# One descriptor per partition for every load of a streaming row normalizer

## The chip, the cores and the metric

The kernel runs on one core of one Trainium2 chip. The metric is the device time of one execution in microseconds (us), lower is better. TensorE is not used. The core's 16 DMA engines carry all traffic between HBM and SBUF.

## The reference

Every row of 1024 numbers is divided by the sum of its absolute values. There are 32 x 512 = 16384 rows, 64 MiB in and 64 MiB out.

```python
batch, seq, dim = 32, 512, 1024
sums = np.sum(np.abs(x), axis=-1, keepdims=True)
return (x / (sums + 1e-8)).astype(np.float32)
```

## The kernel before

The 16384 rows are laid over 128 partitions, 128 rows for each partition, and cut into 11 tiles. Tiles 0 to 9 hold 12 rows per partition: 12 x 4 KB = 48 KB per partition and 6144 KB in all. Tile 10, the last, holds 8 rows per partition: 32 KB and 4096 KB in all. The rows that one partition gets of one tile lie one after another in HBM, so a tile's row of bytes in a partition is one unbroken run on both sides.

`sbuf` has four buffers of the full tile size (`BUFS = 4`). A tile is loaded into a buffer, worked on in place and stored from it. So load i+4 needs the buffer of tile i, and has to wait until store i has landed in HBM.

The order is written out by hand. SyncE's queue (SP) issues all loads, ScalarE's queue (ACT) issues all stores:

```python
for i in range(BUFS):
    load(i)
for i in range(len(rows)):
    compute(i)
    store(i)
    if i + BUFS < len(rows):
        load(i + BUFS)
```

`compute(i)` calls `normalize`. VectorE (DVE) sums the absolute values of each row (line 47), adds the epsilon (line 54), takes the reciprocal (line 56) and multiplies the tile by it (line 58, all rows in one instruction). In tiles 0, 1, 2, 9 and 10 some rows are instead multiplied one at a time, by VectorE (line 65) or by ScalarE (line 68); the table `split` says how many.

`load` (line 86) and `store` (line 89) are one `dma_start` each. Their argument `max_dma_last_dim` is the largest number of bytes that one DMA descriptor may carry. A descriptor is the order for one contiguous run. With `WHOLE` = 49152 bytes a full tile is 128 descriptors of 48 KB, one for each partition. With `HALF` = 24576 bytes it is 256 descriptors of 24 KB, two for each partition. The last tile's 32 KB per partition are one descriptor of 32 KB with `WHOLE`, and two of 16 KB with `HALF`. Every DMA is spread evenly over the 16 engines, 8 partitions for each, so an engine gets 8 or 16 descriptors of each DMA.

Before the change, loads 0 and 1 use `WHOLE` and loads 2 to 10 use `HALF`; stores 0 to 8 use `HALF` and stores 9 and 10 use `WHOLE`.

In the profile q1 is the DMA queue of the loads and q10 that of the stores. What the profile calls a packet is one descriptor; each DMA also has one packet of 4 bytes on each engine, which reports its completion.

Of the kernel before, what the change touches and what calls it, by code (L numbers as in the profile page):

```python
# [1 line left out]

# [4 lines left out]

FP32 = mybir.dt.float32
EPS = 1e-8


@with_exitstack
def kernel(
    ctx: ExitStack,
    tc: tile.TileContext,
    x: bass.AP,
    out: bass.AP,
):
    nc = tc.nc
    P = nc.NUM_PARTITIONS  # L20

    x_flat = x.flatten_outer_dims()
    out_flat = out.flatten_outer_dims()
    n, d = x_flat.shape

    R = 12
    BUFS = 4
    HEAD = 32
    per_partition = n // P
    assert n % P == 0 and (per_partition - HEAD) % R == 0  # L30
    rows = [R] * ((per_partition - HEAD) // R + 2) + [HEAD - 2 * R]

    def piece(flat, i):
        head = flat[: P * HEAD, :].rearrange("(p r) d -> p r d", p=P)
        if i < 2:
            return head[:, R * i : R * (i + 1), :]
        if i == len(rows) - 1:
            return head[:, 2 * R :, :]
        a = P * (HEAD + R * (i - 2))
        return flat[a : a + P * R, :].rearrange("(p r) d -> p r d", p=P)  # L40

    sbuf = ctx.enter_context(tc.tile_pool(name="sbuf", bufs=BUFS))
    stats = ctx.enter_context(tc.tile_pool(name="stats", bufs=len(rows)))

    def normalize(x_tile, k, kv, kt):
        s = stats.tile([P, R], FP32)
        nc.vector.tensor_reduce(  # L47
            out=s[:, :k],
            in_=x_tile[:, :k, :],
            axis=mybir.AxisListType.X,  # L50
            op=mybir.AluOpType.add,
            apply_absolute_value=True,
        )
        nc.vector.tensor_scalar_add(out=s[:, :k], in0=s[:, :k], scalar1=EPS)  # L54
        inv = stats.tile([P, R], FP32)
        nc.vector.reciprocal(out=inv[:, :k], in_=s[:, :k])  # L56
        if kv:
            nc.vector.tensor_mul(  # L58
                out=x_tile[:, :kv, :],
                in0=x_tile[:, :kv, :],  # L60
                in1=inv[:, :kv].unsqueeze(2).to_broadcast([P, kv, d]),
            )
        for r in range(kv, kv + kt):
            row = x_tile[:, r, :]
            nc.vector.tensor_scalar_mul(out=row, in0=row, scalar1=inv[:, r : r + 1])  # L65
        for r in range(kv + kt, k):
            row = x_tile[:, r, :]
            nc.scalar.activation(  # L68
                out=row,
                in_=row,  # L70
                func=mybir.ActivationFunctionType.Copy,
                scale=inv[:, r : r + 1],
            )

    last = len(rows) - 1
    split = {0: (3, 4), 1: (0, 3), 2: (0, 3), last - 1: (0, 2), last: (5, 3)}

    tiles = {}

    HALF, WHOLE = 24576, 49152

    def load(i):
        x_tile = tiles[i] = sbuf.tile([P, R, d], FP32, name="x_tile")
        nc.sync.dma_start(out=x_tile[:, : rows[i], :], in_=piece(x_flat, i), max_dma_last_dim=WHOLE if i < 2 else HALF)  # L86

    def store(i):
        nc.scalar.dma_start(out=piece(out_flat, i), in_=tiles[i][:, : rows[i], :], max_dma_last_dim=WHOLE if i >= last - 1 else HALF)

    def compute(i):
        k = rows[i]
        kt, ks = split.get(i, (0, 0))
        normalize(tiles[i], k, k - kt - ks, kt)

    with tc.manual_schedule():
# [9 lines that stand above are left out]
# [1 line left out]
_INS = ['x']  # L107
_OUTS = [((32, 512, 1024), 'float32')]


# [23 lines left out]
```

## Time and profile before

| what | value |
|---|---|
| time, median of 3 runs | 316.99 us (316.77 to 317.28) |
| span of the profiled execution, from its first to its last instruction | 315.3 us |
| median less span | 1.7 us |
| VectorE busy | 261.2 us (83%) |
| ScalarE busy | 17.4 us (6%) |
| loaded and stored | 67.11 MB each |
| mean DMA rate over the span | 426 GB/s |

The profile does not give a device time of the profiled execution itself; its span stands for it, and the 1.7 us between the span and the median of the timed runs are taken as the same before and after. Busy shares are of the span. The 40 slices of the page are 7.88 us each. In the slices and windows a packet's whole size and time are booked where it starts, so short windows swing by one packet per engine in each direction, and a share can exceed 1.

### The profile page before, as it was taken

What the parts mean: (1) busy time and instruction counts of PE and PEld (TensorE: products, weight loads), DVE (VectorE), ACT (ScalarE), POOL (GpSimd) and SP (SyncE); (2) the same over time, 40 slices, a digit from 0 to 9 for tenths busy, and PEclk for the clock granted to TensorE, in tenths of its full rate; (3) what the DMA queues carried; (4) which work ended last, traced back from release to release, by engine and by line L of the source; (5) the groups of instructions that cost most, each with busy time, mean ns of one, the idle gap of its engine ahead of it and who ended that gap; (6) DMA issues with size and microseconds to landing.
All of it is one profiled execution on the core that took longest, in us unless ns stands there. A gap on an engine that the chain in (4) does not pass through costs nothing.

```text
span 315.3 us, 168 instructions
## 1 busy us (share of the span) xinstructions
DVE 261.2 (83%) x51; ACT 17.4 (6%) x16; POOL 0.2 (0%) x4
## 2 busy tenths in 40 slices
DVE  0079999999999999979996997999699969999100
ACT  0010403004000000000000000000000000203100
POOL 0000000000000000000000000000000000000000
DMA  8999999999999999999999999999999999999997
GB/s 312 486 399 415 433 396 421 430 446 421 430 449 421 427 449 421 427 449 424 427 446 424 427 446 427 424 446 430 421 446 433 421 442 424 441 423 493 399 416 316
DMA packets 5472, 134.22 MB, mean 426 GB/s; under 512 B 352, under 2 KB 352, under 8 KB 352
## 3 DMA queue, kind: packets, MB, share of 16 engines
q1 hardware_dynamic: 2736, 67.11, 49.9%
q10 hardware_dynamic: 2736, 67.11, 49.4%
HBM read 67.11 MB, written 67.11 MB: 426 GB/s over the span
## 4 chain that ended last, share of the span: by engine, by line
DVE 41%; DMA 33%; another core or an unknown queue 18%; SPq 0%; issue 0%; DVEq 0%
DVE s L47 23%; DMA x_tile<-in_x_dram 17%; DMA out_dram<-x_tile 16%; DVE x_tile L58 15%; DVE x_tile L65 2%; DVE inv L56 0%; DVE s L54 0%; SPq L86 0%; DVEq L129 0%
## 5 line engine op out<-in xcount | busy, mean ns | idle before, releaser
L47 DVE TENSOR_REDUCE s<-x_tile 128x12 f32<-128x12288 f32 (+1 forms) x11 | 138.2, 12563 | 30.1 <-DMA x_tile<-in_x_dram 30.1
L58 DVE TENSOR_TENSOR x_tile<-x_tile,inv 128x12288 f32<-128x12288 f32 (+3 forms) x10 | 113.6, 11358 | 0.5
L68 ACT ACTIVATE x_tile<-x_tile,inv 128x1024 f32<-128x1024 f32 x15 | 16.1, 1139 | 257.2 <-DVE inv L56 257.2
L65 DVE TENSOR_SCALAR x_tile<-x_tile,inv 128x1024 f32<-128x1024 f32 x8 | 5.5, 749 | 0.0
L56 DVE RECIPROCAL inv<-s 128x12 f32<-128x12 f32 (+1 forms) x11 | 2.5, 226 | 0.4
L68 ACT ACT_TABLE_LOAD x1 | 1.3, 1283 | 17.8 <-DMA x_tile<-in_x_dram 17.8
L54 DVE TENSOR_SCALAR s<-s 128x12 f32<-128x12 f32 (+1 forms) x11 | 1.9, 173 | 0.4
L118 POOL MEMSET const-bfloat16-1.0<- 128x1 bf16 x1 | 0.1, 102 | 0.0
L118 POOL MEMSET const-uint8-127<- 128x1 uint8 x1 | 0.1, 102 | 0.0
L118 POOL MEMSET const-float32-0.0<- 128x1 f32 x1 | 0.1, 99 | 0.2 <-issue 0.2
L118 POOL MEMSET const-float32-1.0<- 128x1 f32 x1 | 0.1, 99 | 0.0
## 6 DMA issues: line engine op xcount, KB each, us to landing
x_tile<-in_x_dram SPq DMA_DIRECT2D x10, 6144.0 KB, 37.3
out_dram<-x_tile ACTq DMA_DIRECT2D x10, 6144.0 KB, 47.5
x_tile<-in_x_dram SPq DMA_DIRECT2D x1, 4096.0 KB, 32.5
out_dram<-x_tile ACTq DMA_DIRECT2D x1, 4096.0 KB, 21.5
```

The source lines that it names most:

```text
L47: nc.vector.tensor_reduce(out=s[:, :k], in_=x_tile[:, :k, :], axis=mybir.AxisListType.X, op=mybir.AluOpType.add, apply_absolute_value=True,)
L54: nc.vector.tensor_scalar_add(out=s[:, :k], in0=s[:, :k], scalar1=EPS)
L56: nc.vector.reciprocal(out=inv[:, :k], in_=s[:, :k])
L58: nc.vector.tensor_mul(out=x_tile[:, :kv, :], in0=x_tile[:, :kv, :], in1=inv[:, :kv].unsqueeze(2).to_broadcast([P, kv, d]),)
L65: nc.vector.tensor_scalar_mul(out=row, in0=row, scalar1=inv[:, r : r + 1])
L68: nc.scalar.activation(out=row, in_=row, func=mybir.ActivationFunctionType.Copy, scale=inv[:, r : r + 1],)
L118: nc = _bacc.Bacc("TRN2", target_bir_lowering=False, num_devices=1)
```

## The change

Loads 2 to 10 get `WHOLE` as well, so every load has one descriptor per partition. Stores stay as they are: two descriptors per partition for stores 0 to 8, one for stores 9 and 10. No tile, buffer, instruction of VectorE or ScalarE, or order of issue is touched; the instruction lists of both kernels differ in the nine load instructions alone, whose shape goes from 128x2x6144 to 128x12288 (128x2x4096 to 128x8192 for the last).

```diff
     def load(i):
         x_tile = tiles[i] = sbuf.tile([P, R, d], FP32, name="x_tile")
-        nc.sync.dma_start(out=x_tile[:, : rows[i], :], in_=piece(x_flat, i), max_dma_last_dim=WHOLE if i < 2 else HALF)
+        nc.sync.dma_start(out=x_tile[:, : rows[i], :], in_=piece(x_flat, i), max_dma_last_dim=WHOLE)
```

## Prediction, made before the changed kernel ran

> **What bounds the kernel now.** I read the page's busy shares first, then its slices and queues:
>
> ```profile
> span 315.3 us, 168 instructions
> DVE 261.2 (83%) x51; ACT 17.4 (6%) x16; POOL 0.2 (0%) x4
> ...
> DMA  8999999999999999999999999999999999999997
> GB/s 312 486 399 415 433 396 421 430 446 421 430 449 421 427 449 421 427 449 424 427 446 424 427 446 427 424 446 430 421 446 433 421 442 424 441 423 493 399 416 316
> ...
> q1 hardware_dynamic: 2736, 67.11, 49.9%
> q10 hardware_dynamic: 2736, 67.11, 49.4%
> ```
>
> VectorE is idle for a sixth of the span. The DMA row is 9 in every slice but the first and last, and both queues together take 49.9 + 49.4 = 99.3% of the 16 engines' time. The trace's packet records agree: from the first packet at 1.75 us to the last at 313.84 us each engine's packets follow one another with no gap over 40 ns. The page's chain of waits also ends in DMAs: VectorE takes tile after tile as loads land, and loads wait for stores. But it is a chain through instructions; the stores after VectorE's last instruction (292.6 us) run on to 313.84. So the time is the sum of what each engine must move, as long as some queue always has work.
>
> What does a descriptor cost? The DMA view of four windows tells: loads alone in 48 KB pieces (4 to 16.7 us) and in 24 KB pieces (31 to 36.5), both queues in 24 KB pieces (64 to 247), and the last load's 16 KB pieces beside 24 KB stores (257 to 277). Columns are packets, MB, share of 16 engines:
>
> ```profile
> q1 hardware_dynamic: 112, 5.51, 100.1%
> ```
> ```profile
> q1 hardware_dynamic: 112, 2.36, 99.7%
> ```
> ```profile
> DMA packets 3430, 79.23 MB, mean 433 GB/s; under 512 B 206, under 2 KB 206, under 8 KB 206
> ...
> q1 hardware_dynamic: 1714, 39.76, 50.4%
> q10 hardware_dynamic: 1716, 39.47, 50.1%
> ```
> ```profile
> q10 hardware_dynamic: 217, 4.94, 57.3%
> q1 hardware_dynamic: 222, 3.64, 42.4%
> ```
>
> First window: 1.001 x 16 x 12.7 us / 112 = 1.816 us for 48 KB. Second: 0.997 x 16 x 5.5 / 96 data packets = 0.91 us for 24 KB. Starts of successive packets of one engine in the records are finer: 1.812 us for 48 KB, 1.209 for 32 KB, 0.908 for 24 KB, 0.607 for 16 KB. These are the same alone and beside the other queue. So merging two 24 KB pieces saves 2 x 0.908 - 1.812 = 4 to 5 ns (4.4 in means), and two 16 KB pieces 5 ns.
>
> The last two windows tell the arbitration. Beside each other the queues move equal numbers of packets, even where their sizes differ: 222 to 217 packets, 3.64 to 4.94 MB. In the records an engine alternates strictly, one load descriptor, one store descriptor. The Trainium skill, page "DMA: Bandwidth & Descriptors", section on queues, rings and completion order, says instead that an engine drains a whole ring packet of some 9 to 17 descriptors before it turns to the next queue. By that rule the sizes of descriptors would hardly shift the shares; the rows decide against it, and the end time worked out below is the same by both, since it is a sum over a full pipe.
>
> **The change, part by part.** *Descriptors.* Loads 2 to 9 lose 8 descriptors per engine each, 8 x 8 = 64, at 4.4 ns: 0.28 us. Load 10 loses 8 at 5.2 ns: 0.04. Sum: -0.32 us on every engine, all on the path that sets the end. SP's issue instructions cost nothing: their 0.37 us each lies beside full queues.
>
> *Shares.* With loads at 48 KB against stores at 24 KB, a turn of both is 1.812 + 0.908 = 2.72 us and moves twice as much load as store. A load's 8 descriptors per engine need 8 x 2.72 = 21.8 us, and 8 of the 16 store descriptors pass with them; the other 8 run alone, 7.26 us. Together 29.02 us per tile against 32 x 0.908 = 29.06 now: the saving again, nothing more. Loads land sooner, stores later, in the middle of the run.
>
> *Where the VectorE stalls go.* The page shows what VectorE waits for, and the list of waits what SP waits for:
>
> ```profile
> L47 DVE TENSOR_REDUCE s<-x_tile 128x12 f32<-128x12288 f32 (+1 forms) x11 | 138.2, 12563 | 30.1 <-DMA x_tile<-in_x_dram 30.1
> ...
> x_tile<-in_x_dram SPq DMA_DIRECT2D x10, 6144.0 KB, 37.3
> out_dram<-x_tile ACTq DMA_DIRECT2D x10, 6144.0 KB, 47.5
> ```
> ```profile
> SPq L86 <- DMA out_dram<-x_tile: 227.0, 7, 55.3
> ```
>
> 17.7 us of VectorE's 30.1 are the first load; the other 12.4 are five waits for loads 5 to 9. Load latency falls from 37.3 to about 23 us (21.8 plus about 1 from issue to first packet, as for load 0: 0.73 to 1.75), so those waits should almost go. I carried this through with VectorE's durations of the timeline (a middle tile is 12.95 + 12.96 + 0.5 = 26.4 us). Store 0, issued at 38.8, lands about 76 instead of 73, because it gets a third of the pipe until load 3 is in at about 72. From there load i+4 is issued at 76, 105, 134, 163, 193, 222, 251 and lands 23 us later (18 for the last). VectorE runs from tile to tile and ends near 281 instead of 292.6. Late next is the store queue: stores 8, 9 and 10 are then still to move, and the engines end by the sum.
>
> *Is the pipe always full?* A store must already be issued when the one before lands. Store 1 is issued at 61.9 and store 0 lands at 76: 15 us of cover. Later ones have 20 to 34 us, and store 10, issued near 281, is due near 304. So I charge nothing for it; if the cover were gone, each us of late store would cost a us.
>
> *A price the trace does not show.* Now the load queue never runs dry until the last load: load i+4 is issued about 8 us before the one ahead of it lands (load 5 at 102.1, load 4 lands 110.4). After the change load i+4 is issued some 4 to 6 us after load i+3 has landed, from load 4 on, 7 times: the load queue starts from empty while stores run. The nearest rows are two starts from empty. The first packets of load 0 took 2.45 us and 1.8 to 2.8 in all instead of 1.815, on average 0.64 us lost per engine. And when store 0 joined, the load packets around it took up to 1.9 us instead of 0.912, 0.91 us lost per engine on average (the only such place in the trace); the windows view has it at 40 to 44 us (last column GB/s):
>
> ```profile
> 32.00:40.00 8.00, 8.00 (x5) 3.46 (x4) 0.00 (x0) 1.00 1.01 436
> 40.00:44.00 4.00, 4.00 (x1) 0.00 (x0) 0.00 (x0) 1.00 0.95 313
> ```
>
> A restart can cost from 0 to 0.91 us. I take 0: the engine has store descriptors to run while the new queue's first data are on their way, and the loss at 40 us may belong to the first writes to HBM, which occur once in both kernels; load 0's loss had no other work to cover it. Below zero is excluded, since a full pipe has nothing to give back. The Trainium skill, page "HBM Reference", section Latency, speaks against the change: it gives 0.2 us for an access on average and 2 us at high load. If every restart showed that 2 us in full, 7 of them would be 14 us by an estimate from that page; no row here shows a loss that large.
>
> Sum: 315.3 - 0.32 = 315.0 us of span, and with the 1.7 us around it 316.7.
>
> **The rivals.** *Faster.* The stall at 40 us could shrink too, since half as many load descriptors are in flight when store 0 joins. All of it is 0.91 us: 316.99 - 0.32 - 0.91 = 315.8. For it: it is load packets that stretch there. Against it: bytes in flight are the same. Nothing else on the engines is left to gain, since they have no gaps.
>
> *Slower: restarts of an emptied load queue.* Price 7 x c - 0.32. With c = 0.64 (load 0) it is +4.2, 321.2 us; with c = 0.91 (store 0) +6.1, 323.1. It decides from c = 0.046 us for the sign and from (0.63 + 0.32) / 7 = 0.14 us for a loss above 0.2%. For it: both starts from empty in the trace lose time, the second of them beside a queue that was full. Against it: one had nothing to overlap with, the other was the run's first store.
>
> *The change does nothing:* the first two loads already show packets of 49152 bytes under this setting, so it will act. If not, 317.0.
>
> **How the numbers follow.** A measurement of this kernel can tell about 0.2% (0.63 us) from no change. Full pipe with free restarts, 316.7: 0.47, and no effect 0.02; both within 0.2%. Restarts at 0.14 us or more: 0.40. The stall at 40 us also shrinks enough to pass 0.2%: 0.11. So faster 0.11, same 0.49, slower 0.40. The range goes from the faster rival's 315.8 to the slow one's upper bound, 323.1, and leaves out under 1 in 10; the likeliest case alone is 316.3 to 317.2.
>
> **What would show it.** Right: q1 falls from 2736 packets by 72 x 16 = 1152 to 1584, load latency from 37.3 to near 23 us, VectorE's waits for loads from 30.1 to about 18 to 19 us with its last instruction near 281, load packets of 1.815 us also where stores run, and an end of packets near 313.5. Wrong: packets longer than 1.83 us (load) or 0.92 us (store) after 74, 103 or 132 us, where a load begins again, or slices below 9 in the DMA row.

## The result and the profile after

The changed kernel takes 324.31 us (median of 4 runs, 323.44 to 327.93) against 317.05 us before: a ratio of 1.0253, 95% interval 1.0219 to 1.0288. That is 7.3 us slower, and above the upper end of the predicted range. The profiled execution has a span of 321.9 us, 6.6 us more than before. Its page:

```profile
span 321.9 us, 168 instructions
...
DMA  8999999999999999999999999999999999999993
GB/s 336 446 397 483 391 382 446 421 415 437 440 440 434 428 421 434 425 418 428 437 415 382 440 437 458 388 440 406 437 415 440 409 421 430 428 434 458 417 426 143
...
q1 hardware_dynamic: 1584, 67.11, 49.6%
q10 hardware_dynamic: 2736, 67.11, 48.5%
...
L47 DVE TENSOR_REDUCE s<-x_tile 128x12 f32<-128x12288 f32 (+1 forms) x11 | 138.2, 12561 | 30.9 <-DMA x_tile<-in_x_dram 30.9
...
x_tile<-in_x_dram SPq DMA_DIRECT2D x10, 6144.0 KB, 28.7
out_dram<-x_tile ACTq DMA_DIRECT2D x10, 6144.0 KB, 53.3
```

q1 has the 1584 packets that the change was to bring. The DMA row is still 9 from the second slice to the last but one, so it is not idle time that was added. But the last slice is 3 with 143 GB/s where it was 7 with 316, and loads take 28.7 us to land, not the 23 expected.

The chain of waits shows when it happens. SP issues a load each time a store has landed; each piece called "another core or an unknown queue" here is SP's wait for that store, on this one core:

```profile
106.07 0.33 SPq L86
...
106.47 29.80 another core or an unknown queue
...
136.35 0.33 SPq L86
136.67 30.04 another core or an unknown queue
...
166.78 0.33 SPq L86
167.11 29.59 another core or an unknown queue
...
196.76 0.33 SPq L86
197.09 30.30 another core or an unknown queue
...
227.45 0.33 SPq L86
227.78 29.48 another core or an unknown queue
...
257.31 23.47 DMA x_tile<-in_x_dram
```

Before, these steps were 29.0 to 29.1 us apart:

```profile
160.28 0.37 SPq L86
160.65 28.69 another core or an unknown queue
...
189.41 0.37 SPq L86
189.78 28.58 another core or an unknown queue
...
218.43 37.34 DMA x_tile<-in_x_dram
```

Load 4 is issued at 77.04 and load 5 at 106.07, 29.03 us later, the 29.02 of the sum. The five steps that follow are 30.28, 30.43, 29.98, 30.69 and 29.86 us. Six steps take 180.3 us where the sum had 174.1.

The packet records split the 6.6 us in two. Before, no engine has a gap between packets in the middle of the run; after, a few gaps of under 0.9 us come to about 0.15 us per engine in all. So lost time shows almost only as packets longer than their normal length. Summed over packets after 60 us and divided by 16 engines, this stretch is zero before and 3.36 us after. By load, counted from its issue to the next load's issue:

| load that starts again | 4 | 5 | 6 | 7 | 8 | 9 | 10 |
|---|---|---|---|---|---|---|---|
| lost per engine, mean, us | 0.00 | 0.26 | 0.57 | 1.02 | 0.57 | 0.65 | 0.29 |
| from issue to its first packet, us | 3.56 | 3.57 | 3.81 | 4.33 | 3.40 | 4.05 | 3.54 |

All but 0.03 of the 3.36 us fall between 1.5 us before and 9 us after a load's first packet. The rest of each load, another 12 us or more with the same two to one share of loads and stores, loses nothing.

With 0.3 us more at the two starts that the trace of before has too (load 0, store 0), and 0.32 us less for descriptors, the mean engine ends 3.4 us later: 316.99 after, 313.58 before (times at which the 16 engines complete the last store).

The other half is that the engines lose unequally. At load 5 five of them lose 0.3 to 1.4 us each, the others 0.1 or nothing. Followed from packet to packet (each starts where the one before it on its engine ended), the same five lose most again at load 6 (1.3 to 1.6 us against 0.3 or less) and at load 8 (1.0 to 1.3 us against 0.5 or less). After 60 us they lose 5.7 to 6.6 us each, the other eleven 1.4 to 2.8. Each engine has its own 8 partitions of every tile, and what one falls behind is not made good: store 1 completes on all 16 within 0.5 us, store 3 within 2.9, store 5 within 4.6. Before, the last store's 16 completions lie between 313.27 and 313.83 us; after, between 314.79 and 320.44. The slowest engine is 3.45 us behind the mean, where it was 0.25. Together 3.4 + 3.2 = 6.6 us. The windows view of the end shows the engines dropping out one by one (last two columns: DMA share, GB/s):

```profile
308.00:314.00 6.00, 0.00 (x0) 0.00 (x0) 0.00 (x0) 1.00 1.00 431
314.00:320.00 6.00, 0.00 (x0) 0.00 (x0) 0.00 (x0) 1.00 0.39 169
```

### The profile page after: what moved, and what is told of

It is laid out like the page before. It is cut to its first block, busy times and chain, and to the rows that moved or that the text cites. A ratio compares the mean times of both kernels' runs of the same rounds, so it can differ in the third digit from the quotient of the medians.

```text
span 321.9 us, 168 instructions
## 1 busy us (share of the span) xinstructions
DVE 261.1 (81%) x51; ACT 17.4 (5%) x16; POOL 0.2 (0%) x4
## 3 DMA queue, kind: packets, MB, share of 16 engines
q1 hardware_dynamic: 1584, 67.11, 49.6%
## 4 chain that ended last, share of the span: by engine, by line
another core or an unknown queue 46%; DMA 26%; DVE 17%; SPq 1%; issue 0%; DVEq 0%; ACTq 0%
DMA out_dram<-x_tile 14%; DMA x_tile<-in_x_dram 13%; DVE s L47 11%; DVE x_tile L58 5%; DVE x_tile L65 1%; SPq L86 1%; DVE inv L56 0%; DVEq L129 0%; DVE s L54 0%; ACTq L89 0%
## 5 line engine op out<-in xcount | busy, mean ns | idle before, releaser
L47 DVE TENSOR_REDUCE s<-x_tile 128x12 f32<-128x12288 f32 (+1 forms) x11 | 138.2, 12561 | 30.9 <-DMA x_tile<-in_x_dram 30.9
## 6 DMA issues: line engine op xcount, KB each, us to landing
x_tile<-in_x_dram SPq DMA_DIRECT2D x10, 6144.0 KB, 28.7
```

The costliest lines, as they stand in the source:

```text
L47: nc.vector.tensor_reduce(out=s[:, :k], in_=x_tile[:, :k, :], axis=mybir.AxisListType.X, op=mybir.AluOpType.add, apply_absolute_value=True,)
```

## The experiments

Three theories stood against one another. **A**: a load queue that has run empty and starts again beside running stores costs time. **B**: 48 KB packets beside the other queue's packets stretch by themselves. **C**: the two to one share costs by itself, whether or not the queue ran empty.

**All loads and stores with 48 KB.** Same load packets as the changed kernel, but equal shares, so the load queue never runs empty.

```diff
-        nc.scalar.dma_start(..., max_dma_last_dim=WHOLE if i >= last - 1 else HALF)
+        nc.scalar.dma_start(..., max_dma_last_dim=WHOLE)
```

> Theory A (restart): what costs time is a load queue that has run empty and starts again beside running stores. With 48 KB for loads and stores alike the queues share the engines evenly again, load i+4 is queued about 7 us before the load ahead of it is done, and the load queue never runs empty. Then only the descriptor savings are left: 0.32 us of the loads and as much of stores 0 to 8 (9 x 8 x 4.4 ns), so about 316.3 us, and the engines finish within 1 us of one another. Theory B (size): 48 KB load packets beside another queue's packets are themselves what stretches. Then this kernel has as many of them in the mix and is slow as well, 321 us or more.

317.4 us, ratio 1.0011 (1.0002 to 1.0020). Packets after 60 us are stretched by 0.04 us per engine in all. The DMA view from 64 to 247 us, of the changed kernel first and then of this one (packets, MB, share):

```profile
q10 hardware_dynamic: 1715, 39.79, 50.7%
q1 hardware_dynamic: 870, 38.04, 49.4%
```
```profile
q1 hardware_dynamic: 912, 40.11, 50.6%
q10 hardware_dynamic: 910, 39.32, 49.6%
```

In each, 96 packets of q1 are completions of 4 bytes. So a 48 KB load packet took 0.494 x 16 x 183 / 774 = 1.87 us in the changed kernel and 0.506 x 16 x 183 / 816 = 1.82 us here, its length when alone. B falls. C is not touched, since the shares are equal here too. The 0.64 us expected from fewer descriptors did not show in the time: about 0.5 us of it went into more stretch before 45 us (the loads alone and store 0's joining), and one engine ended 1.0 us behind the mean.

**Half the sizes, same shares.** Loads 24 KB, stores 12 KB:

```diff
-        ... max_dma_last_dim=WHOLE if i >= last - 1 else HALF)   # stores
+        ... max_dma_last_dim=WHOLE if i >= last - 1 else HALF // 2)
```

> Loads 24 KB, stores 0 to 10 12 KB (8 KB in the last): no packet is larger than before, but loads again get twice the share of stores and the load queue runs empty before each of loads 4 to 10. Theory A: as slow as the changed kernel, plus 0.6 us for the 144 or more extra store descriptors per engine at 4.4 ns: about 322 to 328 us, with restarts that lose 0.2 to 1 us each and engines that end some 5 us apart. Theory B: no 48 KB packet stands in the mix, so about 317.8 us.

The diff leaves stores 9 and 10 at 48 and 32 KB; the expectation named them wrongly. 319.33 us, ratio 1.0074 (1.0060 to 1.0088): slower, between the two predictions. The load queue is empty before each of loads 4 to 10 again. The losses are 0, 0.02, 0.26, 0.23, 0.20, 0.27 and 0.32 us, 1.3 us in all, and the engines end within 0.9 us of one another. So a 48 KB packet is not needed for a loss. But restarts cost less than half as much with packets of half the size, and the engines hardly part. A's figure for this run was too high.

**Loads held back.** The sizes of the kernel before, with GpSimd work between a store's landing and the next load, so that the queue should run empty at equal shares; and a control where the load does not wait for that work.

```diff
+        if i >= BUFS:
+            nc.gpsimd.memset(x_tile[:, 0, 0:1], 0.0)
+            for _ in range(DELAY):                    # DELAY = 18
+                nc.gpsimd.memset(pad[:, :], 0.0)      # pad is 128x1024, 0.95 us each
+            nc.gpsimd.memset(x_tile[:, 0, 0:1], 0.0)  # not in the control
```

> Packet sizes and shares of the kernel before, but loads 4 to 10 are held back after the landing of their store by 18 memsets of 128x1024 on the otherwise idle GpSimd (about 10 to 20 us), so that the load queue runs empty before each of them. VectorE still has its tiles in time: stores are queued 20 us ahead. Theory A: seven restarts from empty, 3 to 8 us over before, 320 to 325 us. Theory B, or a theory by which the uneven 2 to 1 share is what costs: within 0.3% of before, 316.5 to 318 us.

> Control for the late loads: the same 18 memsets on GpSimd, but the load waits only for a one-column memset ahead of them, so the load queue is as full as before (as long as GpSimd is done with one batch before the next store lands). Both theories: as before within 0.2%, 316.4 to 317.7 us. If it is slower, GpSimd's writes cost DMA time by themselves and the late-load run has to be read against this one.

Late loads 318.47 us, ratio 1.0050 (1.0033 to 1.0067); control 317.34, 1.0015 (1.0006 to 1.0024). This run did not do what it was made for. With no load beside it, a store lands sooner, the next load is issued sooner, and the loads bunch up: in its profile the load queue was empty before load 4 and, for 2.7 us, before load 8, and the store queue before store 4. None of the three shows a loss (0.02 us per engine up to 285 us). It tells only that a restart can be free, not that it is.

**Part of the change alone.** 48 KB for loads 2 and 3 only, and for loads 2 to 6 only:

```diff
-        ... max_dma_last_dim=WHOLE if i < 2 else HALF)   # loads
+        ... max_dma_last_dim=WHOLE if i < 4 else HALF)   # i < 7 in the second
```

> One part of the change alone: loads 2 and 3 with 48 KB descriptors, loads 4 to 10 with 24 KB as before. Load 3 is in at about 73 us, store 0 lands near 76, so load 4 starts an empty queue; from load 5 on the queue is full again. One restart instead of seven. Theory A: a seventh of the loss or less, 0.2 to 1 us: 317.0 to 318.0 us, losses in packets near 80 us only. Theory C: the share is two to one only from 43 to 72 us, where the changed kernel showed no loss: 316.9 us.

> A larger part: loads 2 to 6 with 48 KB descriptors, loads 7 to 10 with 24 KB. Restarts from empty at loads 4, 5, 6 and 7 (about 80, 110, 139 and 168 us), none after that. Theory A: about four sevenths of the loss of 7 us, 319.5 to 321.5 us, packet losses at these four places and none later, engines 3 to 4 us apart at the end. Theory C: three loads (4 to 6) at two to one, about three sevenths, 319 to 320.5 us, and no loss where load 7 with 24 KB begins.

Two loads: 317.08 us, ratio 1.0008 (0.9998 to 1.0017), one restart, 0.04 us lost there: less than A had expected for a start, and a time that fits A and C alike. Five loads: 320.7 us, ratio 1.0111 (1.0092 to 1.0130), four restarts. They lose 0, 0.18, 0.30 and, at load 7, 0.20 us, then 0.17 us more while load 7 runs, and nothing after 195 us. The slowest engine ends 3.4 us behind the mean. Load 7 has 24 KB packets and an equal share, and its start is as dear as those of loads 5 and 6: that speaks against C. Restarts against time go 0, 1, 4, 7 to 316.9, 317.1, 320.7 and 324 us.

**The gap filled.** The last way is to leave sizes and shares of the changed kernel and keep the load queue from running empty. Behind each of loads 3 to 9 small filler loads are queued, 512 bytes per descriptor, into spare tiles that nobody uses. They take turns with store packets until the next load is there.

```diff
+    def filler(i):                     # after load(i), i = 3 to 9
+        for j, (parts, at) in enumerate(((P, 0), (P // 2, 128))):
+            pad = spare.tile([parts, 128], FP32, name=f"pad{i}_{j}")
+            nc.sync.dma_start(out=pad[:, :], in_=x_flat[:parts, at : at + 128])
```

> The changed kernel, with two small filler loads queued right behind each of loads 3 to 9: 192 descriptors of 512 bytes, 12 on each of eight engines and 8 or more on most, read from the first rows of the input into a spare tile that nobody uses. Alternating with store packets of 0.908 us they keep the load queue from running empty for 7 to 11 us until load i+4 is there, and cost about 12 x 0.03 us x 7 = 2.5 us at most. Share and sizes are those of the changed kernel. Theory A (restart from empty costs): the restart losses go, packets after 105 us stay at 1.815 and 0.912 us, the engines end within 1.5 us of one another, time 317 to 319.5 us. Theory C (the two to one share of 48 KB loads and 24 KB stores costs by itself, whether or not the queue ran empty): 324 us or more.

> Control: the same filler loads in the kernel before, whose load queue is never empty. The price of the fillers alone: 0.5 to 2.5 us over before, 317.5 to 319.5 us, by every theory.

323.03 us, ratio 1.0195 (1.0180 to 1.0210), and the control 325.9, 1.0309 (1.0249 to 1.0369). Both times missed what was expected, because the fillers were too long: 12 turns each, on all engines, held the loads themselves back. Load 10 landed at 294 us, VectorE waited 45.1 us for loads instead of 30.9, and the store queue stood empty from 263 to 267 us and from 285 to 296 us. The control, whose queue was full without them, has a starved VectorE too and is no price of the fillers. What can be read is the part before the starving: from 60 to 124 us, where the changed kernel restarts loads 4 and 5, hardly a packet is stretched (0.01 us per engine), with 48 KB loads and 24 KB stores taking turns as in the changed kernel. Later in the run 1.0 us per engine is lost.

With 8 turns:

> The changed kernel with one filler load of 128 descriptors of 512 bytes (8 per engine) behind each of loads 3 to 9, shorter than in the filler run before, whose 12 turns per tile held the loads themselves back. 8 turns beside 0.908 us stores are 7.4 us, just the time in which the load queue of the changed kernel is empty, so a tile again takes 16 turns of either queue, as in the kernel before. The fillers cost 8 x 0.025 x 7 = 1.4 us of engine time. Theory A (restarts): 317 to 319 us, no packet after 60 us over 1.83 (load) or 0.93 us (store) or few of them, engines within 2 us of one another at the end. Theory C (the two to one share itself): 324 us or more.

324.98 us, ratio 1.0256 (1.0242 to 1.0270): nothing gained. The profile shows it load by load. Counting 3.5 us from issue to first packet, loads 4 to 8 were due between 1.3 us after and 0.4 us before the first engine ran out of fillers; loads 6 and 7 lose 0.9 us each, loads 4, 5 and 8 under 0.1. Which of these five lose does not follow from that timing: loads 4 and 7 were both 1.2 to 1.3 us late. Loads 9 and 10 were due 2.5 and 5 us before their fillers ended, and lose nothing: 0.05 us from 227 us to the end. In the changed kernel these two lost 0.65 and 0.29. But the engines had come apart by then, and one ended 5.1 us behind the mean.

With 9 turns:

> The changed kernel once more with fillers, now 9 turns (8 + 1 descriptors of 512 bytes per engine) behind each of loads 3 to 9. With 8 turns the fillers ended just ahead of the next load's first packet at loads 4 to 8, and loads 6 and 7 lost 0.8 us each, while loads 9 and 10, that arrived in time, lost nothing; with 12 turns nothing was lost, but the loads came late and VectorE starved. 9 turns are 8.4 us against the 7.3 us that the queue is empty in the changed kernel, and hold loads back by about 1 us per tile, which VectorE can bear. Theory A (restarts): packets after 60 us almost all at their normal length, engines within 2 us of one another at the end, 317.5 to 320 us (1.6 us of it for the fillers). Theory C (the two to one share itself): 324 us or more.

320.75 us (319.4 to 321.36), ratio 1.0125 (1.0108 to 1.0142), 3.6 us under the changed kernel though it moves 63 descriptors of 512 bytes per engine more, 0.027 us each. In its profile, of the fastest execution (319.4 us), the engines end within 0.5 us of one another, and packets after 60 us are stretched by 1.0 us per engine instead of 3.4. The DMA view shows the one place with a large loss (113 to 121 us, load 5, 0.90 us; load 8 loses 0.1), and a stretch without any, load 6 and its fillers (145 to 176):

```profile
span 317.8 us, 182 instructions
```
```profile
q1 hardware_dynamic: 54, 2.06, 69.6%
q10 hardware_dynamic: 45, 1.11, 33.1%
```
```profile
q10 hardware_dynamic: 303, 7.05, 52.8%
q1 hardware_dynamic: 304, 6.36, 47.6%
```

In the first, 2.06 MB are 42 packets of 48 KB (and 12 small ones), which took 0.696 x 16 x 8 / 42 = 2.1 us each, not 1.815. In the second, 6.36 MB of loads and 7.05 of stores in 31 us are 433 GB/s, the full rate. A holds for the other arrivals; but load 5 did lose, though by its issue time (106.08 us) it was due 3 us before the filler ended. On every engine two store packets pass between its last filler and its first load packet, as many as at load 4, which had less notice (4.8 us from issue to first packet against 7.7) and lost nothing. So either this start took more than twice the usual 3.5 us, or a queue that has not run empty can lose as well; the profile does not decide.

**The mirror image.** Loads from load 2 on 24 KB, all stores 48 KB (32 KB in the last):

> The mirror image: 24 KB loads beside 48 KB stores. Now stores get two thirds; the store queue runs empty before most stores, the load queue does not until late. Theory A as a rule for either queue: several us slower than before, 320 to 326 us. Theory A for load restarts alone (reads that must start from nothing): about as before, 316.5 to 318 us. Theory C: as slow as the changed kernel.

328.81 us, ratio 1.0402 (1.0344 to 1.0459), the slowest of all. The store queue has no packet for 3.7 to 17.5 us before each of stores 3 to 9, and packets after 60 us are stretched by 5.7 us per engine. Part of the rest is starving, as loads now get a third: VectorE waits 54.1 us. So it is not load queues alone that lose. C would make this run slow as well, so it does not part A from C; and how the 11.9 us part between restarts and starving is not settled.

**The changed kernel again**, for a second profile:

> The changed kernel once more, for a second profile: does the first restart (load 4, about 80 us) again cost nothing and the later ones 0.2 to 1 us, and do other engines lose it each time? Theory A: 323 to 328 us, losses right after the load queue starts again and nowhere else beyond the one near 41 us, engines that end several us apart.

323.84 us (322.3 to 327.27), ratio 1.0187 (1.0166 to 1.0207). The seven restarts lose 0.25, 0.53, 0.71, 0.72, 0.49, 0.49 and 0.36 us, 3.6 us in all, and the last store completes between 314.51 and 321.37 us on the 16 engines. The sum is much the same, and 3.28 of the 3.57 us fall again between 1.5 us before and 9 us after a load's first packet. Load 4, free in the first profile, loses here; but it is the cheapest start of all seven, and it lost 0, 0.04 and 0 us in the runs with half the sizes, two loads and five loads. So the first start on an empty queue is mostly free, and the later ones seldom are.

Taken together: restarts of an empty load queue in the changed kernel lost time 13 times of 14 (0.25 to 1.02 us per engine). The loss lies at the start of a load and not in the rest of it, at the same share, which speaks against C; 48 KB packets at equal shares are not stretched, which speaks against B. Loads that were queued behind a longer backlog in the same shares lost nothing in nearly all cases, with one clear exception, and 9 turns of fillers took off 3.6 of the 7.3 us. That starts on an emptied queue bring most of the loss is shown by what goes with them and goes without them. They are not enough by themselves: the size of the packets counts (0.48 and 0.51 us per start with 48 KB loads beside 24 KB stores, 0.19 with 24 beside 12 KB, and 0, 0, 0.04 and 0.20 in the four starts with 24 KB in both queues), and the first start is mostly free. What in the chip takes the time, what decides whether a start loses, why some engines lose and others not, and why smaller packets lose less stays open.

## Why the prediction was wrong

- **The full pipe, the descriptor sum, the alternation: right as far as they went.** 1152 packets of q1 are gone, a turn is one packet of each queue, loads 4 and 5 are issued at 77.0 and 106.1 us (76 and 105 expected), and no store was late. The first cycle took 29.03 us against 29.02. The descriptors' 0.32 us is there, and is nothing beside the rest.
- **The price that the trace does not show: this step failed.** "A restart can cost from 0 to 0.91 us. I take 0." The place and the number of restarts were right, and the average cost lay within the bounds: 0.48 us in the first profile, 0.51 in the second (a single start up to 1.02). But of the two rows that were near, both starts from empty had lost time (0.64 and 0.91), and only reasons were set against them, none of them a row. Their own values would have given 321 to 323 us.
- **"Price 7 x c": mis-sized.** It took the mean engine's loss for the time. With the measured 0.48 us it gives 3.0 us, and 7.3 were measured. The end is set by the slowest of 16, and the losses fell mostly on the same five engines and added up there. The spread at the end, 0.6 us before and 5.7 after, cost as much (3.2 us) as the mean loss (3.4). That put the time above the slow rival's own upper bound of 323.1. The trace had this in it: at 40 us, where store 0 joined, the loss was between 0.7 and 1.5 us by engine, and the prediction used the mean of 0.91.
- **VectorE's waits: wrong.** They were to fall from 30.1 to 18 or 19 us with the end near 281; they are 30.9 us and its last instruction ends at 293.4. An issue needs 3.4 to 4.3 us to its first packet when stores are running, not the 1.0 of load 0. So the load queue stood without a packet for 5.3 to 8.7 us, although load i+4 was issued 1.0 to 3.9 us after load i+3 had landed and not 4 to 6. Each load was then stretched and waited for its slowest engine. It costs nothing by itself: stores 9 and 10 are issued 10 us and more before their turn.
- **The faster rival** got nothing: the loss where store 0 joins is 1.15 us, not less than 0.91.

## What to carry to other kernels

Where loads wait for stores to free their buffers, giving the loads a larger share of the DMA engines does not shorten the run. Each load lands sooner after its issue (28.7 us instead of 37.3 here), but the next one still waits for a store, the load queue runs empty, and a new start beside the running stores can cost up to a microsecond per engine. Keep equal descriptor sizes on two queues that run side by side, so that each has the next transfer queued before it runs dry; the 8 us of the kernel before were enough, where a start on an empty queue took 3.4 us and more to its first packet. And where work is split over 16 engines without rebalancing, price a disturbance by the slowest engine, not by the mean.

## What the runs showed of the hardware beyond that

- The first packet of a DMA came 1.0 us after its issue on idle engines (load 0), and 3.4 to 4.7 us after it on an empty queue while the other queue was running.
- The loss can begin with packets of the running queue: at load 7 of the changed kernel all 16 engines show one store packet of 0.95 to 1.34 us instead of 0.912, and then one or two of their first load packets take 2.0 to 2.8 us. At loads 5 and 8 almost all of it (all but 0.02 to 0.03 us) is in load packets.
- Filler descriptors of 512 bytes hold a place in the alternation as well as 48 KB ones (304 packets of q1 to 303 of q10 from 145 to 176 us with 9 turns): here a queue's share of turns did not depend on what a turn moves.
